# A two-layer sequence trunk on one core: rooms for late weight units, residual rows behind chunks, and two stage ends tied

## The chip, the core and the metric

The kernel runs on one core of a Trainium2 chip. The engines are TensorE (PE, matrix products), VectorE (DVE), ScalarE (ACT), GpSimd (POOL) and SyncE (SP, which issues most of the transfers). The metric is the device time of one execution in microseconds (us); the kernel before takes 2356.06 us, the median of three runs (2353.3 to 2358.04).

## The reference

A sequence of 1024 positions and 1024 channels, in float32, goes through two layers. A layer is: a token mixer on the normed sequence, a feed-forward block, and an embedding gated by the sequence. Each is added to the residual `h`, and one norm ends the program:

```python
for i in range(DEPTH):                                   # 2
    hn = rmsnorm(h, norm_mix_g[i])
    mix = s5_mixer(hn, ...) if i % 2 == 0 else shortconv_mixer(hn, ...)
    h = h + mix
    h = h + swiglu_ffn(rmsnorm(h, norm_ffn_g[i]), ffn_w_in[i], ffn_w_out[i])
    gate = jax.nn.sigmoid(rmsnorm(h, norm_ple_g[i]) @ ple_w_gate[i])
    h = h + gate * (p[i] @ ple_w_up[i])
return rmsnorm(h, final_norm_g)

# s5_mixer ends in a GLU: (z @ w_glu) split in val, gate -> val * sigmoid(gate)
# shortconv_mixer: b, c, v = split(u @ w_in, 3); (b * conv3(c * v)) @ w_out
# swiglu_ffn: gate, up = split(u @ w_in, 2); (silu(gate) * up) @ w_out, hidden 2816
```

## The kernel before

Products run as three: each float32 operand is split into a high part, rounded by a cast on ACT, and a low part, the rest, by a subtraction on DVE (`split`, line 86), and `mm3` (line 121) multiplies high by high, high by low and low by high into one PSUM bank. So PE's lines 122 to 124 are nearly all of its work. The sequence lies in eight row tiles of 128 positions, `h[0]` to `h[7]`, 128x1024 each, and is always walked in `ORDER` (line 65): 0, 4, 1, 5, 2, 6, 3, 7.

The stages follow each other in this order: S5 with its GLU (`glu`), feed-forward in and out of layer 0, the gated embedding (`ple` 0), `conv_in`, `conv_out`, feed-forward in and out of layer 1, `ple` 1 with the final norm.

The in-stages (`ffn_in`, `conv_in`) compute two column blocks at a time by a scheme of seven block products instead of eight (`block_product`, line 289). Its first operand is a set made of two raw loads of columns (`weights_set`, line 258): differences and sums on DVE (lines 275 to 283) and splits into tiles `ws`. Its second operand is the whole normed and transposed sequence, as seven "moving parts" of each pair of row tiles (q, q+4), kept in `ulow` and `uhigh`. Making them is the work of `norm_pair` (line 207): norm two tiles (`normed`; its multiplication is line 173, its result `xn`), transpose them on PE (line 181) into PSUM, form differences on DVE (lines 221 to 232) and split each. A product of a set needs the same moving part of all four pairs. The hidden result goes to DRAM (`hid`), and `h` is parked there too (`spill`, line 235), since the room is needed.

The out-stages (`out_phase`, line 326) run over groups of weight units: `ffn_out` has 22 units in groups 0 to 7, 8 to 15 and 16 to 21, `conv_out` 8 in two groups of four. In a group, each row tile loads its chunks of the hidden (`ch<-hid`, line 346), in the first group also its row of `h` (`h<-hd`, line 348), multiplies and adds to `h` (line 360). A unit is one raw load and one split into a "room": a low slot of `ulow` (`room_low`), a high slot of `uhigh` (`room_high`) or a buffer of its own (`room_new`). Units of the next group marked True are fetched one per row tile in the loop, those marked False after it. Units 18 to 21 are marked False, in high slots 0 to 3, which units 8 to 11 hold until the second group ends. Raw loads, chunks and normed tiles share four raw slots, r0 to r3, taken in turn; a load into a slot waits until its last reader is done.

After a row tile's last sum its `post` runs: after an FFN, `norm_tile`, which norms and transposes the tile for `ple`; after glu, conv_out and ple 0, `norm_pair` for pair t-1 at t = 1, 2, 3, and for pair 3 at t = 7 (`posted`, line 1010).

The order on each engine is a list scheduler's: it records operations in program order, ranks them by priority (`first` raises it for sums and norms) and emits one fixed order per engine, in which the engine then works. SP issues its transfers in its own fixed order too, and waits in it for each slot to be free.

Of the kernel before, what the change touches and what calls it, by code (L numbers as in the profile page):

```python
# [18 lines left out]
P = 128  # L19
# [4 lines left out]
def trunk(  # L24
# [102 lines left out]
    squares = {}  # L127

# [3 lines left out]
    def square(t, cs):  # L132
# [6 lines left out]
        A.activation(junk[:, cs], h[t][:, cs], AF.Square, scale=1.0 / math.sqrt(D), accum_out=ms)  # L139
# [67 lines left out]
    def norm_pair(q, gb):  # L207
        t0, t1 = q, q + HT
        halves = 2 if q == HT - 1 else 1
        x0, x1 = normed(t0, gb, halves), normed(t1, gb, halves)  # L210

        def put(c, src):
            split(moving_part(c, 0, q), moving_part(c, 1, q), by_kt(src))

        p11, p12, p22 = transposed(x0, 0), transposed(x1, 0), transposed(x1, 1)
        p21 = transposed(x0, 1, mm)
        put(0, p11)
        b12 = t2_tile("b12")
        A.copy(b12, p12)
        T1 = t2_tile("T1")  # L220
        V.tensor_tensor(T1, b12, p11, ALU.subtract)
        T2 = t2_tile("T2")
        V.tensor_tensor(T2, p22, T1, ALU.subtract)
        put(1, T2)
        put(2, T1)
        put(3, p21)
        T3 = t2_tile("T3")
        V.tensor_tensor(T3, p22, b12, ALU.subtract)
        put(4, T3)
        put(5, p22)  # L230
        T4 = t2_tile("T4")
        V.tensor_tensor(T4, p21, T2, ALU.subtract)
        put(6, T4)
# [55 lines left out]
    def block_product(ws, on_c11=None):  # L289
# [9 lines left out]
        prod(a, 0, True)  # L299
        s1 = ev_tile("s1")  # L300
# [25 lines left out]
    def out_phase(wout, groups, last_post, following=()):  # L326
# [5 lines left out]
        units = {ht: fetch(ht, room) for ht, room, _ in groups[0]}  # L332
        for gi, group in enumerate(groups):
# [5 lines left out]
            for t in ORDER:  # L339
                parts = {}  # L340
                for ht, *_ in group:
                    if ht // 4 not in parts:
# [3 lines left out]
                        nc.sync.dma_start(out=ch[:, ks].bitcast(F32), in_=hid[ht // 4][t, :, ks])  # L346
                if gi == 0:
                    nc.sync.dma_start(out=h[t], in_=hdram[t])
                ps = [psum() for _ in range(2)]
                for j in parts:  # L350
                    mine = [x[0] for x in group if x[0] // 4 == j]
                    for nb in range(2):
# [5 lines left out]
                        if mine[-1] == group[-1][0]:  # L358
                            with first():
                                V.tensor_tensor(h[t][:, cs], ps[nb], h[t][:, cs], ALU.add)  # L360
# [739 lines left out]
```

## Time and profile before

| what | value |
|---|---|
| median of three runs | 2356.06 us (2353.3 to 2358.04) |
| the profiled execution, its span | 2359.43 us, 2357.5 us |
| PE, DVE, ACT, POOL busy | 2247.0, 1331.9, 765.5, 163.1 us |
| mean granted PE clock | 0.981 |
| moved by DMA | 288.87 MB, mean 123 GB/s |

The span is from the first to the last instruction of the profiled execution, some 2 us less than its time. "Busy" counts work, not waiting; matmuls overlap their neighbours, so a busy PE row ends when the next one may begin. The granted clock is 1.00 or about half of it in any stretch of this trace; the mean over a window tells how much of the window was slow. In a list of waits a row is "engine, tile and line, what it waited for: us in all, times, longest"; in a timeline a row is start, duration, engine, line, operation, output<-input, shape, count and in brackets the idle time before it with what ended it; the chain of waits gives start, duration and step. Rough times of the stages in the span: glu to 407, ffn_in 0 420 to 848, ffn_out 0 to 1110, ple 0 to 1206, conv_in from 1225, conv_out 1463 to 1558, ffn_in 1 from 1571, ffn_out 1 2000 to 2250, ple 1 to the end.

### The profile page before, as it was taken

To read this page: it belongs to the slowest core of one execution; us is meant where nothing else is said; L and a number is where in the kernel's file an instruction comes from. 1 tells how busy PE (TensorE), PEld (TensorE's weight loads), DVE (VectorE), ACT (ScalarE), POOL (GpSimd) and SP (SyncE) were. 2 spreads that over 40 slices of the span, in tenths; PEclk is the share of its full clock that TensorE was granted. 3 is DMA by queue.
4 is the path that set the end of the run, shared out by engine and by line. 5 is a ranking of instruction groups with operands and counts; after the bars stand their busy time and mean duration, and the time that the engine had idled before them with its cause. 6 is when DMAs were issued, how large, how long until landed. Compare 5 with 4: busy or idle time off the path is not lost.

```text
span 2357.5 us, 27090 instructions
## 1 busy us (share of the span) xinstructions
PE 2247.0 (95%) x10253; PEld 1835.7 (78%) x10253; DVE 1331.9 (56%) x2246; ACT 765.5 (32%) x1449; POOL 163.1 (7%) x268
## 2 busy tenths in 40 slices
PE   6888999899999999999979999989999999999998
PEld 4776887788888878878858888768888888788787
DVE  7785326866666642125488776487666666121454
ACT  6554223433333320013343332153333333000232
POOL 2110001000000000000000000010000001000000
PEclk8999999999999999999989999999999999999999
DMA  7555202333333364333232225434333335543333
GB/s 246 141 135 148 69 1 89 105 112 112 111 114 110 107 241 149 118 127 114 70 129 81 90 92 179 159 125 125 108 108 107 111 113 172 212 139 107 108 109 110
DMA packets 212978, 288.87 MB, mean 123 GB/s; under 512 B 21360, under 2 KB 152432, under 8 KB 212848
## 3 DMA queue, kind: packets, MB, share of 16 engines
q1 hardware_dynamic: 191520, 212.63, 29.0%
q0 software_dynamic: 20928, 74.47, 10.2%
q8 instruction: 80, 1.31, 0.2%
q14 instruction: 50, 0.41, 0.1%
q10 hardware_dynamic: 400, 0.04, 0.0%
HBM read 190.93 MB, written 79.69 MB: 115 GB/s over the span
## 4 chain that ended last, share of the span: by engine, by line
PE 85%; DMA 6%; DVE 5%; ACT 1%; SPq 1%; issue 1%; POOL 0%; DVEq 0%; POOLq 0%; ACTq 0%
PE psmm L122 27%; PE psmm L124 27%; PE psmm L123 27%; DMA ch<-hid 2%; PE pstr L181 1%; DMA raw<-in_ffn_w_out_dram 1%; DMA tw<-tmp 1%; DVE W L575 1%; DVE gv L925 1%; DMA h<-hd 1%; DVE tmp L575 1%; DVE ulow L88 1%; DVE uhigh L88 1%; PE pstr L874 0%; DVE raw L575 0%
## 5 line engine op out<-in xcount | busy, mean ns | idle before, releaser
L122 PE MATMUL psmm<-ulow,ws 128*128 128x512 f32 x896 | 351.1, 393 | 1.6 <-ACT s L301 1.6
L123 PE MATMUL psmm<-ulow,ws 128*128 128x512 f32 x896 | 350.6, 391 | 0.0
L124 PE MATMUL psmm<-ulow,ws 128*128 128x512 f32 x896 | 350.4, 391 | 0.0
L124 PE MATMUL psmm<-uhigh,ws 128*128 128x512 f32 x672 | 265.3, 395 | 0.0
L122 PE MATMUL psmm<-uhigh,ws 128*128 128x512 f32 x672 | 265.1, 394 | 0.0
L123 PE MATMUL psmm<-uhigh,ws 128*128 128x512 f32 x672 | 264.9, 394 | 0.0
L360 DVE TENSOR_TENSOR h<-psmm,h 128x512 f32<-128x512 f32 x128 | 88.0, 690 | 276.6 <-PE psmm L124 276.6
L88 DVE TENSOR_TENSOR ws<-raw,ws 128x512 fp32r<-128x512 f32 x224 | 153.6, 688 | 117.8 <-ACT ws L87 117.4
L87 ACT CAST ws<-raw 128x512 fp32r<-128x512 f32 x224 | 137.5, 619 | 213.0 <-PE psmm L124 211.2
L122 PEld LDWEIGHTS psmm<-ulow,ws 128*128 128x128 f32 x896 | 169.4, 189 | 39.5 <-ACT s L301 2.9
L123 PEld LDWEIGHTS psmm<-ulow,ws 128*128 128x128 f32 x896 | 169.4, 189 | 36.2
L124 PEld LDWEIGHTS psmm<-ulow,ws 128*128 128x128 f32 x896 | 169.2, 189 | 36.2
L87 ACT CAST ws<-st 128x512 fp32r<-128x512 f32 x168 | 104.0, 620 | 204.4 <-PE psmm L124 189.5
L123 PEld LDWEIGHTS psmm<-uhigh,ws 128*128 128x128 f32 x672 | 126.1, 188 | 30.3
L124 PEld LDWEIGHTS psmm<-uhigh,ws 128*128 128x128 f32 x672 | 126.1, 188 | 30.3
L122 PEld LDWEIGHTS psmm<-uhigh,ws 128*128 128x128 f32 x672 | 126.1, 188 | 29.1
L323 POOL DMA_DIRECT2D hid<-hs x104 | 78.2, 755 | 903.4 <-DVE hs L88 895.4
L122 PE MATMUL psmm<-ulow,ch 128*128 128x512 f32 x320 | 128.4, 401 | 10.8 <-DMA ch<-hid 10.8
L139 ACT ACTIVATE junk<-h 128x512 bf16<-128x512 f32 (+1 forms) x113 | 64.0, 567 | 204.0 <-DVE h L360 104.0
L87 ACT CAST uhigh<-raw 128x1024 fp32r<-128x1024 f32 x36 | 37.2, 1049 | 278.9 <-PE psmm L124 136.7
L123 PE MATMUL psmm<-ulow,ch 128*128 128x512 f32 x320 | 127.6, 399 | 0.0
L124 PE MATMUL psmm<-ulow,ch 128*128 128x512 f32 x320 | 127.5, 398 | 0.0
(240 smaller groups left out, 4238.5 us busy)
## 6 DMA issues: line engine op xcount, KB each, us to landing
hid<-hs POOLq DMA_DIRECT2D x104, 512.0 KB, 4.3
ch<-hid SPq DMA_DIRECT2D x96, 512.0 KB, 3.7
raw<-in_ffn_w_in_dram SPq DMA_DIRECT2D x88, 512.0 KB, 4.4
raw<-in_ffn_w_out_dram SPq DMA_DIRECT2D x44, 512.0 KB, 3.6
hd<-h POOLq DMA_DIRECT2D x24, 512.0 KB, 3.0
h<-hd SPq DMA_DIRECT2D x24, 512.0 KB, 8.7
raw<-in_conv_w_in_dram SPq DMA_DIRECT2D x24, 512.0 KB, 4.0
up<-ev SPq DMA_DIRECT2D x32, 256.0 KB, 3.2
```

The lines of the kernel that those rows point to most:

```text
L87: A.copy(hi, src)
L88: V.tensor_tensor(lo, src, hi.bitcast(F32), ALU.subtract)
L122: PE.matmul(ps, ahi, bhi, start=start, stop=False, skip_group_check=more)
L123: PE.matmul(ps, ahi, blo, start=False, stop=False, skip_group_check=more)
L124: PE.matmul(ps, alo, bhi, start=False, stop=stop, skip_group_check=more)
L139: A.activation(junk[:, cs], h[t][:, cs], AF.Square, scale=1.0 / math.sqrt(D), accum_out=ms)
L181: PE.transpose(pt[:, c * P:(c + 1) * P], xn[:, kt * P:(kt + 1) * P], ident)
L323: nc.gpsimd.dma_start(out=hid[ht // 4][half * HT:(half + 1) * HT, :, ht % 4].rearrange("t p l j -> p t l j"), in_=hs.bitcast(F32))
L360: V.tensor_tensor(h[t][:, cs], ps[nb], h[t][:, cs], ALU.add)
L575: V.tensor_tensor(o, a, b, op)
L925: V.tensor_tensor_scan(gv[:, g, 1:P], dec, sv[:, g, 1:P], 0.0, ALU.mult, ALU.add)
```

## The change

Three things are changed.

**Rooms.** In `ffn_out` units 18 to 21 are marked True and go to low slots q = 2, 3, which units of the first group held. The four first ple units go to high slots 0 to 3 instead of 4, 5, 0, 1, and all are marked True. In the last group of any `out_phase`, tiles 0, 4, 1 and 5 call their `post` in the loop, tiles 2, 6, 3 and 7 only after it (`kept`).

**Rows.** In the first group, the load of `h[t]` is recorded as issued after the tile's chunk loads.

**Tied ends.** At the ends of glu and of ple 0 (`tied`), `load_set` issues the first set of the next stage's columns into r0 and r1 ahead of the last pass, and `weights_set` takes it from `early`. While a set is loaded early, normed tiles alternate between r2 and r3. At t = 3 only tiles 2 and 6 are normed; at t = 7 `last_pairs` transposes them with the request to stand behind the last sum and the last square, norms tiles 3 and 7, forms pair 2's and pair 3's moving parts, and ties PE's transposes of tile 7 behind the first product of the new stage (`held`). Pair 3's norms in conv_out are no longer made in halves.

```diff
@@ -167,6 +168,9 @@
     def normed(t, gb, halves=1, xn=None):
         with first():
             rs = norm_stat(t)
+            if xn is None and early:
+                turn.append(turn.pop(0))
+                xn = raw_tile(turn[-1], name="xn")
             xn = raw_tile(name="xn") if xn is None else xn
             for c in range(halves):
                 cs = slice(c * D // halves, (c + 1) * D // halves)
@@ -205,32 +209,52 @@
         return uhigh[:, c - 4, kt, l, :]
 
     def norm_pair(q, gb):
-        t0, t1 = q, q + HT
-        halves = 2 if q == HT - 1 else 1
-        x0, x1 = normed(t0, gb, halves), normed(t1, gb, halves)
-
-        def put(c, src):
...
+        x0, x1 = normed(q, gb), normed(q + HT, gb)
+        p = {(0, 0): transposed(x0, 0), (1, 0): transposed(x1, 0), (1, 1): transposed(x1, 1), (0, 1): transposed(x0, 1, mm)}
+        put(0, q, p[0, 0])
+        others(q, p)
+
+    def put(c, q, src):
+        split(moving_part(c, 0, q), moving_part(c, 1, q), by_kt(src))
...
-        put(6, T4)
+        V.tensor_tensor(T4, p[0, 1], T2, ALU.subtract)
+        put(6, q, T4)
+
+    done = {}
+    held = []
+
+    def last_pairs(xs, gb):
+
+
+        a, z = HT - 2, HT - 1
+        with tc.issue_after(done["sum"]), tc.issue_after(done["square"]):
+            p = {(0, 0): transposed(xs[a], 0), (1, 0): transposed(xs[a + HT], 0), (1, 1): transposed(xs[a + HT], 1),
+                 (0, 1): transposed(xs[a], 1, mm)}
+            put(0, a, p[0, 0])
+            xs[z], xs[T - 1] = normed(z, gb, 2), normed(T - 1, gb, 2)
+            r = {(0, i): transposed(xs[z], i, mm) for i in range(2)}
+            put(0, z, r[0, 0])
+            others(a, p)
+            n = len(tc.nc.cur_bb.bb.instructions)
+            r.update({(1, i): transposed(xs[T - 1], i) for i in range(2)})
+            held[:] = [i for i in tc.nc.cur_bb.bb.instructions[n:] if i.engine == PE.engine]
+            others(z, r)
 
     def spill(t):
         nc.gpsimd.dma_start(out=hdram[t], in_=h[t])
 
+    early = []
+
+    def load_set(src_a, src_b):
+
+        got = []
+        for i, src in enumerate((src_a, src_b)):
+            raw = raw_tile(i)
+            nc.sync.dma_start(out=raw.rearrange("p (kt n) -> p kt n", kt=KT), in_=src)
+            got.append(raw)
+        early.append(got)
+
+    def ffn_columns(l, ht):
+        win = ffn_w_in[l].rearrange("(kt p) n -> p kt n", p=P)
+        return win[:, :, ht * P:(ht + 1) * P], win[:, :, HID + ht * P:HID + (ht + 1) * P]
+
+    def conv_columns(*at):
+        win = conv_w_in[0].rearrange("(kt p) n -> p kt n", p=P)
+        return [win[:, :, o * D + ct * P:o * D + (ct + 1) * P] for o, ct in zip(at[::2], at[1::2])]
+
     def weights_set(src_a, src_b):
 
 
-        ra = load_raw(src_a, "p (kt n) -> p kt n", kt=KT)
-        rb = load_raw(src_b, "p (kt n) -> p kt n", kt=KT)
+        ra, rb = early.pop() if early else [load_raw(src, "p (kt n) -> p kt n", kt=KT) for src in (src_a, src_b)]
         a11, a12, a21, a22 = ra[:, 0:512], ra[:, 512:D], rb[:, 0:512], rb[:, 512:D]
 
         def operand(src):
         prod(a, 0, True)
+        product = next(i for i in reversed(tc.nc.cur_bb.bb.instructions) if i.engine == PE.engine)
+        while held:
+            tc.add_manual_dep(held.pop(), product.name,
+                              mybir.DependencyInfo(mybir.DependencyClass.NoSync, mybir.DependencyReason.DATA),
+                              reason="behind the first product")
         s1 = ev_tile("s1")
         A.copy(s1, a)
         b = psum()
@@ -343,9 +391,10 @@
                         parts[ht // 4] = ch = raw_tile(shape=(P, 4, 2, P), dt=F32R, name="ch")
                         of = [x[0] % 4 for x in group if x[0] // 4 == ht // 4]
                         ks = slice(min(of), max(of) + 1)
-                        nc.sync.dma_start(out=ch[:, ks].bitcast(F32), in_=hid[ht // 4][t, :, ks])
+                        load = nc.sync.dma_start(out=ch[:, ks].bitcast(F32), in_=hid[ht // 4][t, :, ks])
                 if gi == 0:
-                    nc.sync.dma_start(out=h[t], in_=hdram[t])
+                    with tc.issue_after(load.ins):
+                        nc.sync.dma_start(out=h[t], in_=hdram[t])
                 ps = [psum() for _ in range(2)]
                 for j in parts:
                     mine = [x[0] for x in group if x[0] // 4 == j]
@@ -357,15 +406,19 @@
                             mm3(ps[nb], ch[:, 0], ch[:, 1], bhi, blo, ht == group[0][0], ht == group[-1][0])
                         if mine[-1] == group[-1][0]:
                             with first():
-                                V.tensor_tensor(h[t][:, cs], ps[nb], h[t][:, cs], ALU.add)
+                                done["sum"] = V.tensor_tensor(h[t][:, cs], ps[nb], h[t][:, cs], ALU.add).ins
                                 if last:
                                     square(t, cs)
                 if soon:
                     soon.pop(0)()
-                if last:
+                if last and t % HT < HT // 2:
                     last_post(t)
+                elif last:
+                    kept.append(t)
             for f in soon + late:
                 f()
+        for t in kept:
+            last_post(t)
 
     def room_low(q, s):
         return lambda: slot_low(q, s)
@@ -396,7 +449,7 @@
     def ffn_out(l, post, following):
         rooms = [(room_low(q, s), False) for s in range(2) for q in range(HT)]
         rooms += [(room_high(i), True) for i in range(6)] + [(room_new(i), True) for i in range(4)]
-        rooms += [(room_high(i), False) for i in range(4)]
+        rooms += [(room_low(q, s), True) for q in (2, 3) for s in range(2)]
         hts = [(ht, *room) for ht, room in enumerate(rooms)]
         cuts = [0, 8, 16, NHT]
         out_phase(ffn_w_out[l].rearrange("(ht p) n -> ht p n", p=P), [hts[a:b] for a, b in zip(cuts, cuts[1:])], post,
                 units = more
+                if ahead:
+                    ahead()
             for t in ORDER:
                 upt = t2_tile("upt")
                 nc.sync.dma_start(out=upt, in_=updram[l][:, t, cs])
...
                 units.append([a.rearrange("p (kt n) -> p kt n", kt=2) for a in unit_of(rooms[nb][u](), raw)])
+            if nb == 3:
+                ahead()
             for t in ORDER:
                 ps = psum()
                 for kt in range(KT):
...
                 return norm_tile(t, gb)
-            if 0 < t < HT:
+            if 0 < t < HT - 1 or (t == HT - 1 and not tied):
                 pair(t - 1)
-            if t == T - 1:
+            elif t == T - 1 and not tied:
                 pair(HT - 1)
+            elif t == HT - 1:
+                xs.update({i: normed(i, gb) for i in (HT - 2, T - 2)})
+            elif t == T - 1:
+                last_pairs(xs, gb)
+                for i in (HT - 2, T - 2, HT - 1, T - 1):
+                    spill(i)
         return post
 
     def inner(name, make, bufs, extra=()):
...
 
-    def ffn_ple(l, last):
-        units, makers = ple_units(l, 0, [room_high(i) for i in (4, 5, 0, 1)])
-        ffn_out(l, posted(norm_ple_g[l], False), [(i < 2, f) for i, f in enumerate(makers)])
+    def ffn_ple(l, last, ahead):
+        units, makers = ple_units(l, 0, [room_high(i) for i in range(4)])
+        ffn_out(l, posted(norm_ple_g[l], False), [(True, f) for f in makers])
         if last:
             gb = load_gain(final_norm_g)
-            ple(l, units, lambda t: final_tile(t, gb))
+            ple(l, units, lambda t: final_tile(t, gb), ahead)
         else:
-            ple(l, units, posted(norm_mix_g[l + 1], True))
+            ple(l, units, posted(norm_mix_g[l + 1], True, True), ahead)
 
     wsp = stp = evq = hsp = None
-    glu(posted(norm_ffn_g[0], True))
+    glu(posted(norm_ffn_g[0], True, True), lambda: load_set(*ffn_columns(0, 0)))
     release()
     inner("f0", lambda: ffn_in(0), (11, 3, 7, 3))
     outer("f0")
-    ffn_ple(0, False)
+    ffn_ple(0, False, lambda: load_set(*conv_columns(1, 0, 2, 0)))
     release()
     inner("c", conv_in, (8, 3, 6, 2), ("cv",))
     outer("c")
```

What the scheduler makes of it is shown at three places. SP at the start of ffn_out 0; `raw` is a weight unit, `ch` a chunk, `h` a residual row. Before, from the first chunk of the first row tile:

```order
L346 DMA ch<-hid_99 128x1024
L346 DMA ch<-hid_100 128x1024
L100 DMA raw<-in_ffn_w_out_dram 128x1024
L348 DMA h<-hd 128x1024 x2
L346 DMA ch<-hid_99 128x1024
L348 DMA h<-hd 128x1024 x6
L346 DMA ch<-hid_100 128x1024
L346 DMA ch<-hid_99 128x1024
L100 DMA raw<-in_ffn_w_out_dram 128x1024
```

and now:

```order
L394 DMA ch<-hid_99 128x1024
L394 DMA ch<-hid_100 128x1024
L100 DMA raw<-in_ffn_w_out_dram 128x1024
L397 DMA h<-hd 128x1024
L394 DMA ch<-hid_99 128x1024
L394 DMA ch<-hid_100 128x1024
L397 DMA h<-hd 128x1024
L394 DMA ch<-hid_99 128x1024
L100 DMA raw<-in_ffn_w_out_dram 128x1024
L394 DMA ch<-hid_100 128x1024
L397 DMA h<-hd 128x1024
```

The rows stood as two and six in front of the second tile's second chunk; now one follows the chunks of each row tile.

DVE at the end of ple 0; `upt` and the sum `h<-upt,h` belong to ple, `T` are a pair's differences, `ulow` and `uhigh` its splits, `ms` the statistics of a norm. The end of pair 2 and the last sum, before:

```order
L276 TENSOR_TENSOR raw<-raw 128x512
L88 TENSOR_TENSOR uhigh<-T_9008,uhigh 128x4x128
L88 TENSOR_TENSOR uhigh<-pstr,uhigh 128x4x128
L433 TENSOR_TENSOR upt<-psmm,upt 128x512
L88 TENSOR_TENSOR ulow<-psmm,ulow 128x4x128
L88 TENSOR_TENSOR uhigh<-T_9014,uhigh 128x4x128
L278 TENSOR_TENSOR st<-raw 128x512
L435 TENSOR_TENSOR h<-upt,h 128x512
L146 TENSOR_TENSOR ms<-ms 128x1
L173 SCALAR_TENSOR_TENSOR xn<-h,rs,gb 128x512 x2
```

and now:

```order
L320 TENSOR_TENSOR st<-raw 128x512
L488 TENSOR_TENSOR upt<-psmm,upt 128x512
L490 TENSOR_TENSOR h<-upt,h 128x512
L145 TENSOR_SCALAR ms<-ms 128x1 x2
L147 TENSOR_TENSOR ms<-ms 128x1 x2
L88 TENSOR_TENSOR ulow<-pstr,ulow 128x4x128
L177 SCALAR_TENSOR_TENSOR xn<-h,rs,gb 128x512 x2
L225 TENSOR_TENSOR T_9060<-b_9058,pstr 128x512
L177 SCALAR_TENSOR_TENSOR xn<-h,rs,gb 128x512 x2
L88 TENSOR_TENSOR ulow<-psmm,ulow 128x4x128
L227 TENSOR_TENSOR T_9062<-pstr,T_9060 128x512
```

The last sum stood behind pair 2's differences and splits; now it comes ahead of them and of the two last normed tiles.

PE at the end of conv_out; `w,ch` are its products, `ident,xn` transposes, `ulow,ws` the first product of ffn_in 1. Before (the transposes of pair 1 and others stand further up, between products):

```order
L123 MATMUL psmm<-w_10993,ch 128x512
L124 MATMUL psmm<-w_10993,ch 128x512
L181 MATMUL pstr<-ident,xn 128x128 x8
L181 MATMUL psmm<-ident,xn 128x128 x4
L181 MATMUL pstr<-ident,xn 128x128 x12
L122 MATMUL psmm<-ulow,ws 128x512
L123 MATMUL psmm<-ulow,ws 128x512
```

and now:

```order
L123 MATMUL psmm<-w_10993,ch 128x512
L124 MATMUL psmm<-w_10993,ch 128x512
L185 MATMUL pstr<-ident,xn 128x128 x12
L185 MATMUL psmm<-ident,xn 128x128 x8
L185 MATMUL pstr<-ident,xn 128x128 x4
L185 MATMUL psmm<-ident,xn 128x128 x4
L185 MATMUL pstr<-ident,xn 128x128 x16
L122 MATMUL psmm<-ulow,ws 128x512
L185 MATMUL pstr<-ident,xn 128x128 x4
L123 MATMUL psmm<-ulow,ws 128x512
```

Twenty-four transposes followed the last product; now it is 44 ahead of the first one of the new stage, and four behind it.

More of the change, by code (lines that the diff above doesn't have):

```diff
@@ L127, in trunk @@
     squares = {}
+    turn = [2, 3]
     def first():
@@ L414, in ple_units, with ple @@
         return units, [lambda u=u: fetch(u) for u in range(KT // 2)]
-    def ple(l, units, post):
+    def ple(l, units, post, ahead):
         more, makers = ple_units(l, 1, [room_new(i) for i in range(4)])
@@ L434, in ple @@
                         hc = slice(nb * 512 + c0, nb * 512 + c1)
-                        V.tensor_tensor(h[t][:, hc], upt[:, c0:c1], h[t][:, hc], ALU.add)
+                        done["sum"] = V.tensor_tensor(h[t][:, hc], upt[:, c0:c1], h[t][:, hc], ALU.add).ins
                         square(t, hc)
@@ L1008, in release, with posted @@
             pools.pop().release()
-    def posted(gain, pairs):
+    def posted(gain, pairs, tied=False):
         gb = load_gain(gain)
+        xs = {}
         def pair(q):
```

33 lines of the change are left out of this document (15 added, 18 removed).

## The prediction

> **What bounds the kernel now.** I read the page's list of busy times and its chain of waits first, then the list of what TensorE (PE) waits for, then windows around each place where PE stands still, and last the timelines inside them.
>
> ```profile
> span 2357.5 us, 27090 instructions
> PE 2247.0 (95%) x10253; PEld 1835.7 (78%) x10253; DVE 1331.9 (56%) x2246; ACT 765.5 (32%) x1449; POOL 163.1 (7%) x268
> PE 85%; DMA 6%; DVE 5%; ACT 1%; SPq 1%; issue 1%; POOL 0%; DVEq 0%; POOLq 0%; ACTq 0%
> PE pstr L181 <- DVE xn L173: 36.0, 5, 10.7
> PE psmm L122 <- DMA ch<-hid: 19.9, 7, 4.6
> ```
>
> PE is busy for 95% of the span and 85% of the ending chain is its own work. The change removes no product, so it can only win where PE idles or runs at a lower clock. The two waits above are the largest: transposes of a normed tile that VectorE (DVE) delivers late (five waits, 36.0 us) and products whose chunk of the hidden activations arrives late (seven, 19.9 us). The stages around them are these:
>
> ```profile
> 429.00:832.00 403.00, 403.00 (x1756) 329.27 (x1756) 267.06 (x421) 149.64 (x256) 30.02 (x40) 1.00 0.37 108
> 864.50:874.50 10.00, 5.41 (x15) 3.97 (x14) 0.00 (x0) 1.04 (x1) 0.00 (x0) 0.66 0.71 283
> 1039.00:1052.00 13.00, 8.23 (x22) 5.91 (x22) 5.27 (x7) 2.38 (x5) 0.56 (x1) 0.74 0.48 157
> 1470.50:1480.00 9.50, 6.77 (x29) 4.93 (x28) 4.25 (x5) 0.00 (x0) 0.00 (x0) 1.00 1.00 375
> 2014.00:2021.50 7.50, 4.05 (x12) 2.91 (x11) 0.00 (x0) 0.84 (x1) 0.00 (x0) 0.77 0.84 337
> 2179.00:2199.00 20.00, 14.64 (x53) 10.90 (x52) 8.34 (x10) 5.45 (x8) 0.56 (x1) 0.83 0.49 168
> 406.00:429.40 23.40, 12.30 (x55) 9.63 (x54) 20.57 (x36) 12.40 (x25) 1.13 (x2) 0.78 0.49 150
> 1206.00:1234.40 28.40, 12.89 (x53) 9.76 (x52) 24.07 (x40) 13.50 (x27) 2.75 (x6) 0.70 0.48 152
> 1557.00:1577.00 20.00, 9.06 (x42) 7.38 (x41) 16.99 (x30) 12.19 (x25) 1.44 (x2) 0.74 0.43 132
> ```
>
> Columns: the stretch, its length, busy time and count on PE, its weight loads, DVE, ACT, POOL, then granted PE clock, DMA share and GB/s. The first row is a stage without a stall: 403 us for 1756 products, 0.2295 us each at clock 1.00. What a stall costs, its slow clock included, is then a stretch's length less its count times 0.2295: 6.6 (864 to 874), 8.0 (1039 to 1052), 2.8 (1470 to 1480), 4.7 (2014 to 2021) and 7.8 (2179 to 2199). The last three rows are the ends of glu, of ple 0 and of conv_out: PE idles about half, while DVE is busy for 20.57 of 23.4, 24.07 of 28.4 and 16.99 of 20 us. There DVE sets the pace.
>
> **Rows behind chunks.** At the start of ffn_out 0:
>
> ```profile
> 848.97 0.32 SPq L346 DMA_DIRECT2D ch<-hid  x1
> 849.34 3.57 SPq L348 DMA_DIRECT2D h<-hd  x6
> 853.94 1.59 SPq L346 DMA_DIRECT2D ch<-hid  x2
> 848.00:870.00 22.00, 17.41 (x74) 13.89 (x74) 6.74 (x9) 2.31 (x4) 2.05 (x3) 0.94 1.00 381
> 853.94 15.60 DMA ch<-hid
> ```
>
> Six residual rows of 512 KB go out between the first and the second chunk of the second row tile; that second chunk is issued at 853.94 and lands 15.6 us later, when PE goes on. The DMA engines are full all that time (share 1.00, 381 GB/s). Six rows are 3.1 MB, 8.3 us at that rate; the PE wait is 4.6. With one row behind each tile's chunks, ahead of this chunk lie the first row and some chunks and weight units: it is on time. What is late next is a row itself, needed only at its tile's first sum, after 48 products (11.0 us), while a tile's 1 MB of chunks, row and weight unit, 2.1 MB, takes 5.5 us. So both ffn_out stalls go: 6.6 and 4.7. In conv_out a tile has 24 products (5.5 us) for about 1.5 MB, 4.2 us at the 375 GB/s of its window; the margin is small, so I take 2.0 of its 2.8. Ends: 0 if DMA stays the bound, 14.1 if all goes. Sum 13.3.
>
> **Late rooms.** The third group of ffn_out needs six weight units. Four of them are fetched only when the second group has ended, into rooms which that group reads; their loads stand in front of the third group's start:
>
> ```profile
> 1033.29 4.54 DMA raw<-in_ffn_w_out_dram
> 1037.86 1.06 ACT uhigh L87
> 1038.94 1.24 DVE uhigh L88
> 1040.19 5.42 DMA ch<-hid
> ```
>
> A raw load, its cast on ACT and its rest on DVE free the raw slot at 1040.19, and only then does the chunk travel, 5.42 us, until PE can go on. In the changed order all six are fetched in the second group's loop, into low slots that the first group has left; a unit costs ACT 1.06 and DVE 1.24 us, and one of them falls on a row tile of 11 us, where PE is the bound. The stall goes in both stages: 8.0 + 7.8 = 15.8, with 12 as the low end, if the cast of the last unit (1.06 + 1.24) still shows.
>
> This has a price: four of eight norm tiles now come after the loop. In the changed order PE's transposes for them stand between ple products, after the last ffn_out product: 8 at once, then 26 products until the next, and so on. Before, there was no stall there:
>
> ```profile
> 1100.00:1200.00 100.00, 100.00 (x466) 82.45 (x466) 53.59 (x85) 38.36 (x76) 8.31 (x13) 1.00 0.29 98
> ```
>
> PE has 100 of 100 us, DVE 53.59, so DVE has room for four norms of 1.28 us each. The cover is the products of the four tiles already transposed: 24 each, 22 us. I cost it at 0; without cover it is the main rival. For the same reason the earlier ple units, now four in the loop, cost 0.
>
> **Tied pairs and columns ahead.** End of ple 0:
>
> ```profile
> 1205.97 0.39 PE L124 MATMUL psmm<-w,ulow 128*128 128x512 f32 x1
> 1207.80 1.09 PE L181 MATMUL pstr<-ident,xn 128*128 128x128 f32 x8 [1.45 <-DVE xn L173]
> 1211.89 0.80 PE L181 MATMUL pstr<-ident,xn 128*128 128x128 f32 x4 [3.00 <-DVE xn L173]
> 1223.97 1.97 PE L181 MATMUL pstr<-ident,xn 128*128 128x128 f32 x8 [10.39 <-DVE xn L173]
> 1225.59 0.78 PE L122 MATMUL psmm<-ulow,ws 128*128 128x512 f32 x1
> 1210.40 0.69 DVE L221 TENSOR_TENSOR T<-b,pstr 128x512 f32<-128x512 f32 x1 [0.31 <-ACT b L219]
> 1218.33 0.68 DVE L433 TENSOR_TENSOR upt<-psmm,upt 128x512 f32<-128x512 f32 x1
> 1220.72 0.68 DVE L435 TENSOR_TENSOR h<-upt,h 128x512 f32<-128x512 f32 x1
> 1223.17 1.41 DVE L173 SCALAR_TENSOR_TENSOR xn<-h,rs,gb 128x512 f32<-128x512 f32 x2 [0.75 <-POOL cvp L527]
> ```
>
> The last product starts at 1205.97, but its sum runs on DVE only at 1220.72, behind pair 2's differences and splits that begin at 1210.40. Tied, these come behind that sum. I walk the new order at 0.60 us per 128x512 operation (1210.40 to 1218.33 holds eleven of them and a normed tile), 1.41 per tile normed in halves: last sum done 1211.5, square, statistics and pow to 1213.4, both normed tiles with a first difference to 1216.8, splits to 1219.5, the first weights to 1221. The first product starts near 1221.5 instead of 1225.59: gain 4. Its later operands, pair 2's and 3's other parts, still need the same DVE operations, so it may be 1; if they all hide, 6.
>
> At glu the same walk gives less:
>
> ```profile
> 416.19 0.42 DVE L503 TENSOR_TENSOR h<-sgg,h 128x256 f32<-128x256 f32 x1
> 418.15 1.41 DVE L173 SCALAR_TENSOR_TENSOR xn<-h,rs,gb 128x512 f32<-128x512 f32 x2 [0.75 <-POOL rs L148]
> 420.58 0.78 PE L122 MATMUL psmm<-ulow,ws 128*128 128x512 f32 x1
> ```
>
> The first product starts some 3 us earlier, near 417.8. But the set loaded ahead sits in slots r0 and r1, the normed tiles alternate in r2 and r3, so the second set's columns wait until DVE has read the first set, near 423 by this walk; and PE's order puts two products of the second set among the first ones. Counted to the 28th product I get 428.9 against 429.4: 0.5, with ends of -2 and +4. Loading ahead by itself earns nothing: no wait for raw columns shows in either boundary. The end of ple 1 is unchanged: 0.
>
> **What is moved without being tied.** The rule that keeps half of the tiles until after the loop also holds in conv_out, whose pairs are not tied. Pairs 1 and 2 ran beside its products; now they come after the last one.
>
> ```profile
> 1557.18 0.69 DVE L360 TENSOR_TENSOR h<-psmm,h 128x512 f32<-128x512 f32 x1 [0.39 <-PE psmm L124]
> 1568.88 1.42 DVE L173 SCALAR_TENSOR_TENSOR xn<-h,rs,gb 128x512 f32<-128x512 f32 x2 [0.46 <-POOL rs L148]
> 1571.31 0.78 PE L122 MATMUL psmm<-ulow,ws 128*128 128x512 f32 x1
> 1576.58 0.39 PE L123 MATMUL psmm<-ulow,ws 128*128 128x512 f32 x1
> ```
>
> PE reaches its last product some 2.5 us earlier, since 24 transposes (1.04 per 8 elsewhere) leave the loop. From the last sum, near 1555.2, the new DVE order has three normed tiles (1.28 each) and 21 operations at 0.60 to the split that completes the first moving part: 16.7 us, 1571.9, and another 23 operations to the end of pair 3. My walk lets the first product run haltingly and ends the 17th at 1580.6 instead of about 1576.8: a loss of 4, and I take 4.5. The ends: -1, if these operations find gaps; -11, if pair 1's eleven operations (6.6 us) come on top.
>
> **The sum.** 13.3 + 15.8 + 4 + 0.5 - 4.5 = 29.1 us. The profiled execution took 2359.43, its span 2357.5; the median of the runs is 2356.06, 3.4 below. From the median: **2327**.
>
> One rule of the Trainium skill is weighed here. Of my five stall terms the four with a clock under 1.00 hold 6.6, 8.0, 4.7 and 7.8 against idle times of 4.6, 4.8, 3.5 and 5.4 (length less busy): the slow clock adds 2.0, 3.2, 1.3 and 2.5, 9.0 together; the stretch at 1470 with 2.7 idle keeps clock 1.00. TensorE: Matmul & The Clock Gate, "What's actually happening", says that PE's clock halves after an idle window of about 3.4 us and returns after about as long a busy one, the windows running freely. By it such a stall would cost an estimated 1.7 beyond its idle time, 6.8 for the four, and the result would be 2329; this trace agrees on where the clock falls, and its rows say a little more, so they stand.
>
> **The rivals.**
> A, DVE stays the bound at all three ends: tied pairs only change the order of the same operations, so 0 at glu and ple 0, and conv_out loses 11. For it: DVE is busy in 85% or more of those windows. Against: the last sum's 10 us behind pair 2. 29.1 - 4.5 - 6.5 = 18.1: 2338.
> B, the upper ends: +4, +6 and -1: 38.1: 2318. Against it, the same busy DVE.
> C, the chunks stay late: rows and chunks share engines at 375 to 385 GB/s, so a row's load only returns its time elsewhere (sums that wait for a row). 29.1 - 13.3 = 15.8: 2340. Against: 5.5 us of transfer in 11 of product.
> D, the rooms don't do what they say: the third group's chunks still lack a raw slot. 29.1 - 15.8 = 13.3: 2343. Against: six loads over eight row tiles.
> E, the other side: the kept tiles make PE wait. PE works in order; if each kept transposition stands there before its normed tile is done, the end of ple 0 shows the price: 1.45 + 3.00 + 10.39, with about 2.2 for the clock 17 us, once in each ffn_out, and conv_out at -11: 29.1 - 34 - 6.5 = -11.4: 2367. It decides from about 11 us per ffn_out on. Against it: 22 us of products ahead of most of those transposes, and the gapless 100 us.
>
> **How the numbers follow.** Forecast 0.56 (its own range 2321 to 2333), A 0.20, B 0.12, C 0.05, D 0.03, E 0.04. Leaving out E, D in part and the lower tail of B gives 2312 to 2342. A measurement tells 0.2%, 4.7 us, from no change; A to D all lie beyond it: faster 0.93, within 0.03, slower 0.04.
>
> **What would show it.** In the changed profile the waits of products for chunks should fall from 19.9 to under 5 us in all; no stretch under clock 1.00 near ffn_out's start and its second group's end; ple without stalls in its first 40 us; first product of conv_in about 15.5 us after ple's last instead of 19.6; first product of ffn_in 1 some 17.5 after conv_out's last instead of 14.6. I am wrong if PE waits for a row's sum or a kept tile, or if the ends of glu and ple 0 keep their idle time.

## The result and the profile after

The changed kernel takes 2327.98 us, the median of four runs (2326.97 to 2328.67); the kernel before took 2355.07 beside it. The ratio is 0.9883, its 95% interval 0.9866 to 0.99: 23 to 32 us less, against 2327 forecast. The profiled execution has a span of 2325.2 us instead of 2357.5. One execution of a kernel tried below, that of the late rooms alone, took 5766.33 us, with each product at some 0.6 us instead of 0.23; why is not known, and it is left out of that kernel's time.

The page's busy times and chain, and the largest waits of PE, of the changed kernel:

```profile
PE 2245.4 (97%) x10253; PEld 1834.8 (79%) x10253; DVE 1331.9 (57%) x2244; ACT 766.3 (33%) x1449; POOL 161.8 (7%) x268
PE 89%; DVE 6%; DMA 2%; ACT 1%; SPq 1%; issue 1%; POOL 0%; DVEq 0%; POOLq 0%; ACTq 0%
PE psmm L185 <- DVE xn L177: 9.5, 3, 5.2
PE pstr L185 <- ACT b L223: 6.6, 2, 5.2
PE psmm L122 <- ACT ws L87: 3.5, 3, 1.3
```

The products' wait for chunks, 19.9 us before, has no row left in that list, and DMA fell from 6% to 2% of the chain. The wait for normed tiles fell from 36.0 to 10.1 (9.5, and 0.6 in a row further down) and is partly replaced by waits for splits and differences (`b`, `ws`).

The places where PE stood before, in windows of the changed kernel (length, PE, PE weight loads, DVE, ACT, POOL, then granted clock, DMA share, GB/s); first the start of ffn_out 0, the end of its second group, the start of conv_out's flow, the start of ffn_out 1, the end of its second group, and last the ends of glu, of ple 0 and of conv_out:

```profile
842.00:875.00 33.00, 33.00 (x143) 26.56 (x142) 11.51 (x14) 4.74 (x6) 2.06 (x3) 1.00 0.72 260
1015.00:1035.00 20.00, 20.00 (x88) 16.15 (x87) 6.63 (x9) 3.55 (x6) 0.56 (x1) 1.00 0.37 119
1440.00:1462.00 22.00, 22.00 (x96) 17.68 (x96) 10.82 (x14) 4.37 (x5) 2.05 (x3) 1.00 0.82 290
1985.00:2000.00 15.00, 15.00 (x66) 12.06 (x65) 3.30 (x4) 1.05 (x1) 0.56 (x1) 1.00 0.78 282
2150.00:2175.00 25.00, 25.00 (x113) 20.30 (x112) 9.70 (x16) 5.96 (x12) 1.10 (x2) 1.00 0.46 146
403.00:424.40 21.40, 13.20 (x45) 9.69 (x44) 20.56 (x42) 12.94 (x26) 1.63 (x3) 0.68 0.34 104
1186.00:1211.20 25.20, 14.41 (x61) 10.28 (x60) 23.97 (x42) 14.10 (x28) 2.58 (x6) 0.73 0.38 125
1528.00:1556.00 28.00, 15.99 (x69) 12.15 (x68) 27.54 (x44) 17.07 (x32) 2.03 (x2) 0.69 0.31 94
```

The five stalls on transfers are gone, at full clock. At the last three places PE is still idle for about 40% of the time, with DVE busy nearly all of it, and conv_out's end is now the worst.

Since both kernels give PE the same 10253 instructions, the starts of the k-th instruction can be subtracted, stage by stage, at points where both kernels have the same order. The S5 part, which the change does not touch, is 4.2 us shorter in this execution; the rest:

| place | forecast | gained in the trace |
|---|---|---|
| start of ffn_out 0, of ffn_out 1 | 6.6, 4.7 | 7.0, 5.1 |
| chunks of conv_out | 2.0 | 3.2 |
| end of the second groups | 8.0, 7.8 | 8.0, 8.0; 7.3 and 7.4 left in ple |
| end of glu, of ple 0 | 0.5, 4 | 0.6, 4.0 |
| end of conv_out | -4.5 | -6.3 |
| all, from S5's end to the last instruction | 29.1 | 28.1 |

Some expectations below take 0.8 and 4.3 for the ends of glu and ple 0; counted from the last products that come in the same place of both orders, they are 0.6 and 4.0.

### The profile page after: what moved, and what is told of

It is laid out like the page before. It is cut to its first block, busy times and chain, and to the rows that moved or that the text cites. A ratio compares the mean times of both kernels' runs of the same rounds, so it can differ in the third digit from the quotient of the medians.

```text
span 2325.2 us, 27092 instructions
## 1 busy us (share of the span) xinstructions
PE 2245.4 (97%) x10253; PEld 1834.8 (79%) x10253; DVE 1331.9 (57%) x2244; ACT 766.3 (33%) x1449; POOL 161.8 (7%) x268
## 4 chain that ended last, share of the span: by engine, by line
PE 89%; DVE 6%; DMA 2%; ACT 1%; SPq 1%; issue 1%; POOL 0%; DVEq 0%; POOLq 0%; ACTq 0%
PE psmm L122 29%; PE psmm L124 29%; PE psmm L123 29%; DMA tw<-tmp 1%; PE pstr L185 1%; DVE W L632 1%; DVE gv L982 1%; DVE tmp L632 0%; DVE ulow L88 0%; DVE xn L177 0%; SPq L950 0%; PE pstr L997 0%; DMA wraw<-in_ple_w_up_dram 0%; PE pstr L931 0%; DVE ptab L632 0%
## 5 line engine op out<-in xcount | busy, mean ns | idle before, releaser
L123 PE MATMUL psmm<-ulow,ch 128*128 128x512 f32 x448 | 177.2, 396 | 0.0
L122 PE MATMUL psmm<-ulow,ch 128*128 128x512 f32 x448 | 176.9, 395 | 0.0
L124 PE MATMUL psmm<-ulow,ch 128*128 128x512 f32 x448 | 176.9, 395 | 0.0
L122 PEld LDWEIGHTS psmm<-uhigh,ws 128*128 128x128 f32 x672 | 126.1, 188 | 29.1
L88 DVE TENSOR_TENSOR ws<-st,ws 128x512 fp32r<-128x512 f32 x168 | 115.2, 686 | 1.2 <-ACT ws L87 1.1
```

Of the source, the lines that this page charges most:

```text
L88: V.tensor_tensor(lo, src, hi.bitcast(F32), ALU.subtract)
L122: PE.matmul(ps, ahi, bhi, start=start, stop=False, skip_group_check=more)
L123: PE.matmul(ps, ahi, blo, start=False, stop=False, skip_group_check=more)
L124: PE.matmul(ps, alo, bhi, start=False, stop=stop, skip_group_check=more)
```

## The experiments

Each is compared with the kernel before, run on the same chip; ratios have 95% intervals.

**The late posts of conv_out.** Only the test for `kept` is changed:

```diff
-                if last and t % HT < HT // 2:
+                if last and (t % HT < HT // 2 or len(groups) == 2):
```

> The changed kernel, but conv_out calls every tile's post in its loop again, as before; ffn_out keeps the late posts. My theory: the late posts cost conv_out's end 4.5 to 6 us and nothing else there is worse, so the time falls from 2328 to 2322 to 2323.5, the first product of ffn_in 1 again follows conv_out's last one by about 14.6 us, and DVE has pair 1's eleven operations beside the products. Rival: the loss at that end comes from the new order of rows and chunks or from pair 3's norms in one piece instead of halves, not from the late posts; then the time stays within 1.5 us of 2328.

Measured: 2322.71 us, ratio 0.9863 (0.9847 to 0.988), 5.3 less than the changed kernel. The traces agree until conv_out's last products; from there to the flow of ffn_in 1, where its products follow each other without waits, this kernel is 5 us faster (1.4 lost against the kernel before, instead of 6.3). Its end in PE's timeline, and the window that answers to the last row above:

```profile
1531.91 0.66 PE L185 MATMUL pstr<-ident,xn 128*128 128x128 f32 x4
1543.53 1.97 PE L185 MATMUL pstr<-ident,xn 128*128 128x128 f32 x8 [10.96 <-DVE xn L177]
1545.15 0.78 PE L122 MATMUL psmm<-ulow,ws 128*128 128x512 f32 x1
1528.00:1556.00 28.00, 16.36 (x71) 13.24 (x70) 24.72 (x42) 13.86 (x27) 2.00 (x3) 0.76 0.45 137
```

And the end of conv_out in the changed kernel:

```profile
1542.88 0.79 PE L122 MATMUL psmm<-ulow,ws 128*128 128x512 f32 x1
1545.11 1.11 PE L185 MATMUL pstr<-ident,xn 128*128 128x128 f32 x4 [1.44 <-ACT b L223]
1546.88 0.63 PE L122 MATMUL psmm<-ulow,ws 128*128 128x512 f32 x1
1552.96 0.80 PE L122 MATMUL psmm<-ulow,ws 128*128 128x512 f32 x1 [2.96 <-ACT s L348]
```

The changed kernel starts ffn_in 1 no later, but its first products come haltingly and stop again at 1552.96, with DVE busy for 27.54 of 28 us. So the late posts are the cause, as the theory had it; the rival's order of rows and chunks and undivided norms are in both kernels. This version is faster than both kernels.

**Tying conv_out's end as well**, on top of the first experiment:

```diff
-    conv_out(posted(norm_ffn_g[1], True))
+    conv_out(posted(norm_ffn_g[1], True, True))
```

> Like the run with conv_out's posts in its loop, but its last two pairs are tied behind the last sum as at glu and ple 0 (no set is loaded ahead, since chunks need all four raw slots). My theory: what tying earned at ple 0, about 4 us, came from the last sum no longer standing behind pair 2's operations; conv_out's last sum stands less deep (1557.18 against a last product started at 1556.74), so tying earns at most 1 to 2 us there: 2321 to 2323. Rival: tying earns by the order of the splits, wherever it stands, 4 us: 2318.

Measured: 2324.11 us, ratio 0.9871 (0.9855 to 0.9886). No gain: the difference to 2322.71 is within the spread of the runs, and in the trace that end loses 1.7 us, against 1.4 untied. Both readings expected some gain; neither holds. The set that glu and ple load ahead is missing here, which the next experiment bears on.

This trace shows one thing more. Up to 1524 us PE, DVE, ACT and SP work through the same instructions in the same order as in the first experiment. Yet glu's end loses 2.3 us here, where it gained 0.5 there. Late in that end PE goes on after a pause, in the first experiment and here:

```profile
424.02 0.98 PE L122 MATMUL psmm<-ulow,ws 128*128 128x512 f32 x3 [1.57 <-ACT ulow L87]
425.22 1.65 PE L122 MATMUL psmm<-ulow,ws 128*128 128x512 f32 x3 [2.95 <-ACT ulow L87]
```

In the first the clock is 1.00 from 419.6 on; here it came back at 417.6, and after the longer pause it is half again from 424.4 to 431.3. So executions of one order can differ by 2.8 us at a tied end.

**Without the early loads**: the two calls of `ahead()` are taken out, the ends stay tied.

```diff
-                if ahead:
-                    ahead()
...
-            if nb == 3:
-                ahead()
```

> The changed kernel without the two early loads; the first sets of ffn_in 0 and conv_in are loaded as before and normed tiles take the raw slots in turn. My theory: loading ahead earned nothing by itself, since no wait for raw columns showed at these ends: 2327 to 2330. Rival: the early set is what lets DVE make the first differences of the columns before the last sum, and without it the first product waits for them; 4 us at each of the two ends: 2335 to 2337.

Measured: 2334.16 us, ratio 0.9912 (0.9897 to 0.9927): 6 us lost. My theory falls, and the rival holds at one end only: glu's end keeps its gain (0.7 us against the kernel before), ple 0's end turns from 4.0 us gained into 3.2 lost. DVE there, in the kernel without early loads:

```profile
1187.91 1.76 SPq L100 DMA_DIRECT2D raw<-in_conv_w_in_dram  x2
1188.74 0.69 DVE L488 TENSOR_TENSOR h<-upt,h 128x512 f32<-128x512 f32 x1
1196.76 0.69 DVE L317 TENSOR_TENSOR st<-raw 128x512 f32<-128x512 f32 x1 [7.33 <-DMA raw<-in_conv_w_in_dram]
1197.37 0.69 DVE L486 TENSOR_TENSOR upt<-psmm,upt 128x512 f32<-128x512 f32 x1
```

and in the changed kernel:

```profile
1185.24 0.69 DVE L317 TENSOR_TENSOR st<-raw 128x512 f32<-128x512 f32 x1
1188.79 0.68 DVE L490 TENSOR_TENSOR h<-upt,h 128x512 f32<-128x512 f32 x1
1190.71 0.69 DVE L490 TENSOR_TENSOR h<-upt,h 128x512 f32<-128x512 f32 x1
```

Taking pair 2 away from ahead of the last sum brings the set's first difference there, in DVE's fixed order. Its columns are issued only at 1187.91, in a raw slot shared with normed tiles, and the last sum waits 7.33 us behind it. With the early load that difference runs at 1185.24. At glu's end DVE's order has it behind the last sum (at 410.96, the sum at 403.24), so there nothing waits.

**The early loads without tying**, the other half:

```diff
-    glu(posted(norm_ffn_g[0], True, True), lambda: load_set(*ffn_columns(0, 0)))
+    glu(posted(norm_ffn_g[0], True), lambda: load_set(*ffn_columns(0, 0)))
...
-            ple(l, units, posted(norm_mix_g[l + 1], True, True), ahead)
+            ple(l, units, posted(norm_mix_g[l + 1], True), ahead)
```

> The changed kernel with the early loads kept at glu and ple 0, but their last two pairs not tied: pair 2 runs at t = 3 as before. What was seen without the early loads (2334, and 7.3 us of DVE waiting for raw columns at ple 0's end, ahead of the last sum) leaves two readings. One: tying and loading ahead need each other; tied alone the columns come late, ahead alone the last sum stands behind pair 2 again, so ple 0's end loses its whole 4.3 us and glu's 0.8: 2332 to 2334. The other: the early load earns 7 us by itself and tying costs 3, so without tying the time falls: 2325.

Measured: 2331.09 us, ratio 0.9899 (0.9883 to 0.9914), 3.1 more than the changed kernel. In the trace ple 0's end gains 0.7 instead of 4.0, glu's 0.1. The time is 0.9 under the first reading's range and far from the second's; the trace bears the first out: at ple 0 each half needs the other.

**The tied ends and early loads alone**: the changed kernel with rooms, rows and late posts as before:

```diff
-        rooms += [(room_low(q, s), True) for q in (2, 3) for s in range(2)]
+        rooms += [(room_high(i), False) for i in range(4)]
...
-                    with tc.issue_after(load.ins):
-                        nc.sync.dma_start(out=h[t], in_=hdram[t])
+                    nc.sync.dma_start(out=h[t], in_=hdram[t])
...
-                if last and t % HT < HT // 2:
+                if last:
                     last_post(t)
...
```

> The kernel before with only the two tied ends and their early loads (rows and rooms as before, conv_out's posts in its loop). If the parts add: 0.8 us at glu and 4.3 at ple 0, so 2350 to 2351.5. If the ends only paid because other stalls had moved: 2355 or more.

Measured: 2355.35 us, median of eleven runs (2350.74 to 2359.42), ratio 0.9998 (0.9989 to 1.0007). By the number the second reading: the ends earn nothing here. Its reason, that they only paid because other stalls had moved, is not shown. In this trace glu's end loses 0.7 us, ple 0's gains 0.9 and conv_out's, which is not tied, loses 0.9. PE's first products at the tied ends follow the same course as in the changed kernel, but the slow clock comes a second time, for 3.4 us at each of the two ends by the trace's clock records (425.1 and 1230.6), at these pauses:

```profile
425.60 1.65 PE L122 MATMUL psmm<-ulow,ws 128*128 128x512 f32 x3 [2.80 <-ACT ulow L87]
1229.17 0.97 PE L122 MATMUL psmm<-ulow,ws 128*128 128x512 f32 x3 [2.30 <-ACT ulow L87]
```

In the changed kernel's trace PE waits 1.7 us at the first place (423.75), 0.8 and 1.0 at the second (1209.31, 1211.02), and the clock stays. The trace of conv_out's tied end has the same second stretch at glu's end without the five stalls on transfers, so these are not needed for it. That it takes the gain away in most of the eleven executions is likely and not shown, since only one of them has a trace.

**Rows alone**, in the kernel before:

```diff
+                        load = nc.sync.dma_start(...)
                 if gi == 0:
-                    nc.sync.dma_start(out=h[t], in_=hdram[t])
+                    with tc.issue_after(load.ins):
+                        nc.sync.dma_start(out=h[t], in_=hdram[t])
```

> The kernel before with only the residual rows put behind each tile's chunks. My theory: 6.6 and 4.7 us at the starts of the two ffn_outs and 2 to 3 us in conv_out: 2341 to 2343, all of it at those three places, and the waits for chunks at the ends of the second groups unchanged. Rival: the engines are full, the rows' transfers take their time from later chunks or sums, and half of it comes back: 2348.

Measured: 2341.13 us, ratio 0.9939 (0.9924 to 0.9954), 14.6 less. In the trace 7.0, 3.0 and 5.1 us at the three starts, and nothing is given back.

**Rows ahead of their own chunks.** On top of the first experiment, a row is issued just in front of its tile's chunks and behind the tile before; it is still one per tile (`load` is the last chunk load so far):

```diff
+                if gi == 0 and t == 0:
+                    row = nc.sync.dma_start(out=h[t], in_=hdram[t])
+                elif gi == 0:
+                    with tc.issue_after(load.ins):
+                        row = nc.sync.dma_start(out=h[t], in_=hdram[t])
...
+                        if gi == 0:
+                            with tc.issue_after(row.ins):
+                                load = nc.sync.dma_start(out=ch[:, ks].bitcast(F32), in_=hid[ht // 4][t, :, ks])
...
```

> The kernel with conv_out's posts in its loop (2322.7), but each residual row is issued just ahead of its own tile's chunks instead of behind them; rows are still spread, one per tile. My theory: spreading does it, one row of 0.5 MB delays a chunk by 1.4 us at 375 GB/s, which 11 us of products hide in ffn_out and 5.5 us nearly hide in conv_out: 2322 to 2325. Rival: a row in front of a chunk costs the stall again, at least 3 us at each of the three starts: 2329 or more.

Measured: 2341.69 us, ratio 0.994 (0.9928 to 0.9953). By the number the rival wins, but not by the trace:

```profile
830.48 10.16 SPq L100 DMA_DIRECT2D raw<-in_ffn_w_out_dram  x5
840.73 0.38 SPq L390 DMA_DIRECT2D h<-hd  x1
841.29 0.82 SPq L401 DMA_DIRECT2D ch<-hid  x2
846.71 0.76 PE L122 MATMUL psmm<-ulow,ch 128*128 128x512 f32 x1 [4.31 <-DMA ch<-hid]
PE psmm L122 <- DMA ch<-hid: 12.7, 3, 4.6
```

There are three waits in all, each for the very first chunk of a stage. With the row tied in front of it, the scheduler put it behind all nine weight loads, the last of which waits for a raw slot: issued at 841.29. In the changed kernel SP sends it between them, at 837.85:

```profile
831.12 4.34 SPq L100 DMA_DIRECT2D raw<-in_ffn_w_out_dram  x4
837.85 2.06 SPq L394 DMA_DIRECT2D ch<-hid  x2
840.72 0.33 SPq L100 DMA_DIRECT2D raw<-in_ffn_w_out_dram  x1
841.10 0.42 SPq L397 DMA_DIRECT2D h<-hd  x1
```

So the next run, again on top of the first experiment, left the first tile's row behind its chunks and put the other seven ahead:

```diff
+                if gi == 0 and t > 0:
+                    with tc.issue_after(load.ins):
+                        row = nc.sync.dma_start(out=h[t], in_=hdram[t])
...
                 if gi == 0:
-                    with tc.issue_after(load.ins):
-                        nc.sync.dma_start(out=h[t], in_=hdram[t])
+                    if t == 0:
+                        with tc.issue_after(load.ins):
+                            nc.sync.dma_start(out=h[t], in_=hdram[t])
```

> Rows ahead of their own tile's chunks, but the first tile's row behind its chunks, all else as in the kernel at 2322.7. With every row ahead the time was 2341.7; there the first tile's chunks stood behind the ninth weight load in SP's order (issued 841.29 instead of 838.14), and no product waited for a chunk after the first one of a stage. Theory: 0.5 MB more in front of a chunk is hidden, and the loss was the first tile's place in the queue: 2322 to 2324. Rival: a row ahead of a chunk costs by its bytes: 2330 or more.

Measured: 2325.29 us, ratio 0.9874 (0.986 to 0.9887), 2.6 above the first experiment and 1.3 above the theory's range, well under the rival's. Both ffn_out starts keep their 7.0 and 5.1 us. conv_out's gains 1.3 instead of 3.2, with one wait for a chunk of 1.7 us: the only stage where 0.5 MB ahead of a chunk is felt. Spreading the rows earned most of the gain; standing behind the chunk counts at a stage's first tile, and in conv_out.

**Late rooms alone**, in the kernel before, with late posts in ffn_out only and the ple units moved as in the changed kernel; run twice:

```diff
-        rooms += [(room_high(i), False) for i in range(4)]
+        rooms += [(room_low(q, s), True) for q in (2, 3) for s in range(2)]
...
```

> The kernel before with only the late rooms moved and ffn_out's last posts after its loop (conv_out's stay in the loop). My theory: 8.0 and 7.8 us at the ends of the second groups, the late posts free: 2340 to 2341. Rival: the late posts cost each ffn_out's end some us, as they did in conv_out (5): 2345 to 2350.

> The kernel before with only the late rooms moved and ffn_out's late posts, once more, for a trace: 2341 to 2344. If the late posts are free, the ends of the second groups give 7.4 us each in the trace and nothing is lost in the 60 us behind them; if they cost, the trace shows PE waiting for a normed tile in ple's first 40 us.

Measured: 2343.10 and 2343.03 us, ratios 0.9946 (0.9931 to 0.9961) and 0.995 (0.9936 to 0.9963): 12 to 13 us less, under the 15 to 16 of the first expectation and within the second's. In the trace of the second the ends of the two groups gain 8.0 each, of which 7.3 and 7.4 are left in ple; PE's waits in ple's first 40 us do not appear. The late posts are free there. What is missing lies elsewhere: 1.9 us at the start of ffn_out 1, a stall this version keeps, and 1.2 at conv_out's end, which it does not touch either.

**Junk products against the slow clock.** On top of the first experiment, 12, 22 and 44 products are written to an unused PSUM tile in PE's idle stretches at the ends of glu, ple 0 and conv_out:

```diff
+        for k in range(n):
+            PE.matmul(ps, ulow[:, 0, 0:P], ulow[:, 0, 0:512], start=True, stop=True)
```

> The kernel with conv_out's posts in its loop (2322.7), with 12, 22 and 44 junk products of 128x512 written to an unused PSUM tile in PE's idle stretches at the ends of glu, ple 0 and conv_out; everything else stands in the same order. Reading one: the slow clock after the idle stretch costs about 3.5 us at each end (24 or so transposes and products at 0.43 instead of 0.23 us); the junk keeps the clock at 1.00 and 6 to 11 us go: 2312 to 2317. Reading two: DVE sets the pace there, faster products only wait for their splits: 2321 to 2323, with the clock at 1.00 and new waits in the place of the slow products.

Measured: 2321.53 us, ratio 0.9854 (0.9841 to 0.9868), not to be told from 2322.71. The ends of ple 0, glu and conv_out, with the first experiment's kernel first and the junk's behind it:

```profile
1184.00:1212.00 28.00, 17.50 (x74) 12.81 (x73) 25.84 (x46) 15.47 (x31) 3.68 (x7) 0.76 0.40 128
403.00:425.00 22.00, 13.92 (x47) 10.22 (x46) 21.16 (x44) 13.28 (x27) 1.63 (x3) 0.69 0.35 106
1528.00:1555.00 27.00, 15.36 (x66) 12.40 (x65) 23.72 (x41) 13.86 (x27) 2.00 (x3) 0.75 0.47 142
```

```profile
1184.00:1212.00 28.00, 22.35 (x99) 16.55 (x97) 25.83 (x46) 14.04 (x28) 3.69 (x7) 0.88 0.37 122
403.00:425.00 22.00, 16.12 (x71) 12.16 (x69) 20.00 (x41) 11.75 (x24) 1.64 (x3) 0.84 0.32 100
1528.00:1555.00 27.00, 23.87 (x115) 19.03 (x114) 23.34 (x38) 12.92 (x27) 2.15 (x4) 1.00 0.49 154
```

The clock rose to 0.88, 0.84 and 1.00, and DVE had done about the same work when each window ended. Leaving the junk out of the count, the trace gains 0.1, 0.1 and 1.0 us at the three ends. The second reading holds, as far as the clock was raised: DVE sets the pace there, and the slow clock behind the idle stretch mostly fills time in which PE would wait.

## Why the prediction was right, and where it was not

**Rows behind chunks.** 13.3 forecast, 15.3 in the changed kernel's trace, 14.6 alone. Mechanism and size held; conv_out gave all of its stall (3.2), not the 2.0 taken. The argument by bytes was half of it: a row in front of a chunk is indeed hidden in ffn_out, but the first chunk of a stage depends on its place among the weight loads in SP's order, which the prediction did not look at.

**Late rooms.** 15.8 forecast, 14.7 in both traces that have it, 12 to 13 by the medians alone. The late posts in ffn_out cost nothing, as said: rival E has no wait to show. Rivals C and D have none either.

**Tied pairs and early loads.** 4.5 forecast, 4.6 in the trace. The number came out near, but one step of its reasoning failed: "Loading ahead by itself earns nothing: no wait for raw columns shows in either boundary." That the kernel before does not wait said nothing on the order that tying makes. Without the early loads a new wait of 7.33 us stands ahead of the last sum, and 6 us are lost. The prediction costed the two edits apart and looked for what was late only in the old order. The walk was off as well: at ple 0 the first product comes 11.5 us after ple's last one (1185.87 to 1197.38), not 15.5, and what it gains beyond 4 us is given back while the next products wait for splits and run at the slow clock. That the net is 4 is thus partly luck. The size is unsure too: taking tying away costs 3.1 us, adding both to the kernel before gives 0 with an interval of about 2 us either way, and one order differed by 2.8 us between two executions at glu's end.

**conv_out's late posts.** -4.5 forecast; -6.3 in the trace, of which 1.4 stays when the posts go back into the loop; 5.3 by the medians of the first experiment. The cause held. The first product came 15.0 us after conv_out's last one, not 17.5; what was not foreseen is that the flow stops a second time at 1552.96.

**The slow clock.** Where PE waits for a transfer and then flows freely, the slow clock adds to the stall, as the sum had it: 6.6 of which 4.6 idle, and 7.0 came. Where DVE sets the pace the first slow stretch adds almost nothing, as the junk products show; where a second one came, behind the first products, glu's end was 2.8 us longer than in an execution of the same order without it. Rival A's premise, DVE as the bound of the three ends, is thus right; its time was not, since the order of DVE's operations still decides when the first product flows.

The sum owes something to luck: parts tried alone give 14.6 + 12.4 + 0 - 5.3 = 21.7, the whole 27.1. With intervals of 2 to 4 us either way on each, that gap is at the edge of what these runs can tell; whether the parts help each other or the clock's moments differ stays open.

## What to carry to other kernels

A stall's cost on the path is its stretch less its work at full pace, slow clock included, when the engine flows freely behind it; where another engine sets the pace, look at that engine's order first, and at the clock only behind it. When an edit takes operations away from in front of a critical one, list what the fixed order puts there instead, and what that waits for; two edits may have to be made together to earn anything. A rule written for one stage ("the last tiles post late") should be checked in every stage that shares its code: here it cost 5 us of 33 in one.

## What was not expected of the hardware

The starts of the half-speed stretches in the changed kernel's clock records are 405.3, 1190.4, 1535.1 and 1552.2 us: distances of 785.1, 344.7 and 17.1 us, 230, 101 and 5 times 3.413, and the stretches last 13.7, 13.7, 13.7 and 6.8, four and two times as much. So whether a pause of 2 to 3 us slows PE seems to depend on where it falls in a fixed grid of 3.413 us: the pause of 2.30 us up to 1229.17 did in the trace of the tied ends alone, one of 2.20 us up to 1479.82 did not in the kernel before. The Trainium skill gives a reason (TensorE: Matmul & The Clock Gate, "What's actually happening": activity is judged in free-running windows of 3413 ns); the grid in this trace agrees. The pause of 2.30 us that slowed PE was shorter than one such window. The same kernel then need not lose the same at such a pause from one execution to the next, and at glu's end it did not: 2.3 us lost in one, 0.5 gained in the other.
